# The closing norm of a decoder step: each chunk's norm formed under the next chunk's products, in three steps

## The chip, the cores and the metric

One core of a Trainium2 chip runs the whole program. The metric is device microseconds for one execution, from the first to the last instruction and what lies around them; lower is better. The core's engines work side by side, each through its own list of instructions in a fixed order: TensorE (PE) multiplies matrices into PSUM, VectorE (DVE) and GpSimd (POOL) do elementwise work, ScalarE (ACT) does functions and copies, and SyncE (SP) issues the transfers. An instruction that waits holds back everything behind it on its own engine.

## The reference

The program is one layer of a decoder for 1024 prompt tokens and 64 sample tokens (8 sequences of 8), followed by the final norm:

```python
def rms_norm(x, g):
    xf = x.astype(jnp.float32)
    y = xf * lax.rsqrt(jnp.mean(xf * xf, axis=-1, keepdims=True) + EPS)
    return (y * g.astype(jnp.float32)).astype(x.dtype)

def trunk_layer(x, ...):
    h = rms_norm(x, norm_mix_g)
    proj = h @ w_in
    ...                                   # convolution heads, attention heads
    x = x + jnp.concatenate([a, o], axis=-1) @ w_out
    h = rms_norm(x, norm_ffn_g)
    ...
    x = x + (jax.nn.silu(g) * (h @ w_ffn_up)) @ w_ffn_down
    return x, k, v, ...

y_prompt = rms_norm(xp, norm_final_g)
y_sample = rms_norm(xs, norm_final_g)
```

What matters here is the end: the product with `w_ffn_down`, the addition to `x`, and the last `rms_norm`, over 1024 features of each of 1088 tokens.

## The kernel before

Activations lie transposed: features on the 128 partitions (eight tiles `x2[0]` to `x2[7]`, one per 128 features, so `m` runs over 8), the 1088 tokens along the free axis. An f32 product is made of three matmuls: both operands are split into a rounded high part and the remainder (`whi`, `wlo`, `xh`, `xl`), and high times high, high times low and low times high are summed in one PSUM bank.

The product with `w_down` adds over 22 tiles of hidden features, in four groups (`GROUPS`). The first three groups go through `gemm` and are added to `x2`. The last group has two tiles from each half, so four activations, and goes through `last_product`. It takes the tokens in four chunks (`TAIL`: first token and width), and for each chunk the eight feature tiles `m` in turn. One product of a chunk is 12 matmuls into one PSUM bank; the tag `g` has 5 banks, which go round. Then, per `m`:

- DVE adds the bank to `x2[m]` (L1199), which frees the bank;
- ACT squares the sum (L1201) into a tile `sq`;
- the squares are added up over `m` (L1206): odd `m` on DVE, even `m` on POOL, in two running sums, which DVE joins at the end (L1207).

`last_norm` turns the summed squares of a chunk into output. `rstd` first multiplies the sum by a column of ones (L191, tag `r` in the trace), which adds over the partitions and leaves a token's sum in one partition; DVE, ACT and DVE make the inverse root of a few numbers (L193 to L206: tiles `rv`, `rr`, `rt`; L201 is the square root on ACT). Then PE transposes these, spread over 128 columns, back into rows of tokens (L213), and ACT copies them to SBUF (L215: tile `rb`). With `rb` the eight tiles of the chunk are scaled: even `m` by one instruction on DVE (L1215), odd `m` by a product on POOL (L1217) and a scaling on ACT (L1218). SP then issues the transfer of each (L1219).

The order of the work is set in two places. The code is written so that `last_norm` of a chunk comes behind `last_product` of the next chunk. A scheduler that works at build time then arranges each engine's list by what it reckons to be ready; the chip executes that list as it stands. The names `x_1742`, `x_1749`, `x_1774`, `x_1781`, `x_1788`, `x_1795`, `x_1802`, `x_1809` in the lists are `x2[0]` to `x2[7]`.

Of the kernel before, what the change touches and what calls it, by code (L numbers as in the profile page):

```python
# [21 lines left out]
ALU = mybir.AluOpType  # L22
PSUM = bass.MemoryType.PSUM

P = 128
D = 1024
# [4 lines left out]
N = S + NS  # L31
# [10 lines left out]
LN2 = float(np.log(2.0))  # L42
CHUNKS = ((0, 384), (384, 384), (768, 320))
GROUPS = ((0, 3), (3, 3), (6, 3), (9, 2))
TAIL = ((0, 256), (256, 256), (512, 320), (832, 256))
CH = 384
NCH = NCACHE // CH

# [23 lines left out]
C_GMIX, C_GFFN, C_GFIN = 0, 8, 16  # L72
# [5 lines left out]
def trunk_kernel(tc, xT, w_in, w_out, w_gate, w_up, w_down, par, kc, vc, sa, sf, pmask, smask,  # L78
                 yT, kT, vT, ca, cas, cf):
    nc = tc.nc  # L80
    with (
# [8 lines left out]
        def nm(s):  # L90
            cnt[0] += 1
            return f"{s}_{cnt[0]}"
# [20 lines left out]
        def bank(z, tag, bufs):  # L113
            return zone[z + "ps"].tile([P, 512], F32, tag=tag, name=nm(tag), bufs=bufs)
# [20 lines left out]
        def col(c):  # L135
            return prm[:, c:c + 1]
# [44 lines left out]

        rooted = [None]

        def rstd(sq, div, new, width=N):


            ps = bank(*rbank[0])
            nt = -(-width // P)
            size = [min(P, width - i * P) for i in range(nt)]
            for i, n in enumerate(size):  # L190
                nc.tensor.matmul(ps[:n, i:i + 1], sq[:, i * P:i * P + n], ones, start=True, stop=True)  # L191
            v = sp.tile([P, 9], F32, tag="rv", name=nm("rv"), bufs=2)[:, :nt]
            nc.vector.memset(v, 1.0)  # L193
            nf = width // P
            nc.vector.tensor_scalar(v[:, 0:nf], ps[:, 0:nf], 1.0 / div, EPS, op0=ALU.mult, op1=ALU.add)
            if nf < nt:
                n = size[-1]
                nc.vector.tensor_scalar(v[:n, nf:nt], ps[:n, nf:nt], 1.0 / div, EPS, op0=ALU.mult, op1=ALU.add)
            r = sp.tile([P, 9], F32, tag="rr", name=nm("rr"), bufs=2)[:, :nt]
            nc.vector.reciprocal(r, v)  # L200
            nc.scalar.activation(r, r, AF.Sqrt)  # L201

            t = sp.tile([P, 9], F32, tag="rt", name=nm("rt"), bufs=2)[:, :nt]
            nc.vector.tensor_mul(t, r, r)
            nc.vector.scalar_tensor_tensor(t, t, -0.5, v, op0=ALU.mult, op1=ALU.mult)
            rooted[0] = nc.vector.scalar_tensor_tensor(r, t, 1.5, r, op0=ALU.add, op1=ALU.mult).ins  # L206
            rb = new("rb")
            for c0 in range(0, width, 512):
                pb = bank(*rbank[0])
                w = min(512, width - c0)  # L210
                for i in range(c0 // P, -(-(c0 + w) // P)):
                    n = size[i]
                    nc.tensor.transpose(pb[:, i * P - c0:i * P - c0 + n], r[:n, i:i + 1].to_broadcast([n, P]),  # L213
                                        ident[:n, :n])
                nc.scalar.activation(rb[:, c0:c0 + w], pb[:, :w], AF.Copy)  # L215
            return rb

        def sum_squares(xs, eng, new, pool=()):
            acc = new("sqa")
            nc.scalar.activation(acc, xs[0], AF.Square)  # L220
            for i, x in enumerate(xs[1:]):
                s = new("sq")
                if i + 1 in pool:
                    nc.gpsimd.tensor_mul(s, x, x)
                else:
                    nc.scalar.activation(s, x, AF.Square)
                eng.tensor_add(acc, s, acc)
            return acc
# [517 lines left out]
        i = 0  # L746
        for p in range(NS1, NP):
            prompt_heads(i, HEADS[p - NS1])
            i = HEADS[p - NS1]
# [55 lines left out]
        for p, upto in zip(range(NS1, NP), SHEADS):  # L805
            prompt_heads(i, upto)
            i = max(i, upto)
# [46 lines left out]
        n = PARTS[-1]  # L854
# [11 lines left out]
        for m0 in (0, 4):  # L866
# [3 lines left out]
            for i in range(2):  # L870
                r = raw[:, i * 512:i * 512 + 512]
# [61 lines left out]
        for i in range(2):  # L933
            x = first_up[0][:, i * half:i * half + half]
# [5 lines left out]
        def out_half(h, hook):  # L940


            c = slice(h * HN, h * HN + HN)
            for m in range(KT):
                ps = pair()
                block_product(ps, wl[m], part[h], True)
                x = x2[m][:, c]
                added = nc.vector.tensor_add(x, all_of(ps), x).ins
                nc.sync.dma_start(x2d[m][:, c], x)
                s = slot("t1", "sq", F32)  # L950
                nc.scalar.activation(s, x, AF.Square)
                if m == 0:
                    acc = s
                else:
                    added = nc.vector.tensor_add(acc, s, acc).ins
                hook(m, added)
            return acc, added
# [5 lines left out]
        def norm_half(sq):  # L963
            return rstd(sq, D, lambda s: slot("t3", s, F32), HN)
# [16 lines left out]
        sq1, added = out_half(1, norm_first)  # L981
# [141 lines left out]
        def wide(s, dt=F32):  # L1123
            return zt("D", "X", ACTS, s, N, dt)
# [61 lines left out]
        nj = len(act)  # L1186


        def last_product(t0, n):
            acc = [None, None]  # L1190
            for m in range(KT):
                ps = bank(*gbank[0])
                whi, wlo = w[m]
                for k, (xh, xl) in enumerate(act):
                    nc.tensor.matmul(ps[:, :n], whi[:, k, :], xh[:, t0:t0 + n], start=(k == 0), stop=False)
                    nc.tensor.matmul(ps[:, :n], whi[:, k, :], xl[:, t0:t0 + n], start=False, stop=False)
                    nc.tensor.matmul(ps[:, :n], wlo[:, k, :], xh[:, t0:t0 + n], start=False, stop=(k == nj - 1))
                x = x2[m][:, t0:t0 + n]
                nc.vector.tensor_add(x, ps[:, :n], x)  # L1199
                s = wide("sq")[:, :n]  # L1200
                nc.scalar.activation(s, x, AF.Square)  # L1201
                i = m % 2
                if acc[i] is None:
                    acc[i] = s
                else:
                    (nc.vector if i else nc.gpsimd).tensor_add(acc[i], s, acc[i])  # L1206
            nc.vector.tensor_add(acc[0], acc[1], acc[0])  # L1207
            return acc[0]

        def last_norm(acc, t0, n):  # L1210
            R3 = rstd(acc, D, wide, n)[:, :n]
            for m in range(KT):
                x = x2[m][:, t0:t0 + n]
                if m % 2 == 0:
                    nc.vector.scalar_tensor_tensor(x, x, col(C_GFIN + m), R3, op0=ALU.mult, op1=ALU.mult)  # L1215
                else:
                    nc.gpsimd.tensor_mul(x, x, R3)  # L1217
                    nc.scalar.activation(x, x, AF.Copy, scale=col(C_GFIN + m))  # L1218
                nc.sync.dma_start(yT[m * P:(m + 1) * P, t0:t0 + n], x)  # L1219

        sums = []
        for i in range(len(TAIL)):
            sums.append(last_product(*TAIL[i]))
            if i:
                last_norm(sums[i - 1], *TAIL[i - 1])
        last_norm(sums[-1], *TAIL[-1])
        zd.__exit__(None, None, None)
        zr.__exit__(None, None, None)

# [91 lines left out]
```

## Time and profile before

| | us |
|---|---|
| median of three runs | 1429.69 (1428.96 to 1431.0) |
| the profiled execution's own time | 1432.72 |
| its span, first to last instruction | 1430.9 |
| products of the four chunks, within the span | 1362.25 to 1412.36 |
| behind the last product | 1412.36 to 1430.90 |

Times inside the span are read from its start. A row of the timeline gives start, duration, engine, source line, operation and shapes; equal neighbours are merged into one row with a count, and then the duration runs from the first one's start to the last one's end. What stands in brackets is the idle time before it and what ended it. A matmul's duration is longer than the distance to the next, because matmuls are pipelined: the distance is the pace.

### The profile page before, as it was taken

How to read it: one execution, taken by the hardware profiler on the slowest of the kernel's cores; microseconds unless marked ns; L12 is line 12 of the kernel's file. 1: busy time of each engine (PE TensorE's matmuls, PEld its weight loads, DVE VectorE, ACT ScalarE, POOL GpSimd, SP SyncE). 2: the span in 40 equal slices, each digit the busy share in tenths (PEclk: the TensorE clock that was granted, in tenths of full speed). 3: DMA queues.
4: the chain of work that ended last, by engine and by line, in shares of the span. 5: the costliest groups of instructions: out<-in, count | busy, mean ns of one | idle time of the engine just before them, and what ended most of it. 6: DMA issues, size and time to landing. Idle time of an engine off the chain costs nothing.

```text
span 1430.9 us, 24745 instructions
## 1 busy us (share of the span) xinstructions
PE 1350.0 (94%) x10011; PEld 1280.5 (89%) x10011; DVE 861.0 (60%) x1649; ACT 514.3 (36%) x982; POOL 431.5 (30%) x303
## 2 busy tenths in 40 slices
PE   6999999999999998976999999999999999999995
PEld 6988889999977777876899999999999889999995
DVE  7398595566574665679756566655656642423146
ACT  5312211457565564345333323333332321212033
POOL 3221111110000115231454445545445211224124
PEclk9999999999999998987999999999999999999998
DMA  7246676746699887340022122122212571414003
GB/s 271 54 139 245 226 255 206 206 141 179 180 276 226 243 228 225 112 162 8 30 91 91 65 87 91 52 70 91 91 62 91 167 291 45 139 48 131 11 9 118
DMA packets 84882, 195.16 MB, mean 136 GB/s; under 512 B 12576, under 2 KB 46752, under 8 KB 84768
## 3 DMA queue, kind: packets, MB, share of 16 engines
q1 hardware_dynamic: 84768, 193.57, 42.8%
q8 instruction: 79, 1.29, 0.4%
q14 instruction: 35, 0.29, 0.1%
HBM read 145.03 MB, written 48.52 MB: 135 GB/s over the span
## 4 chain that ended last, share of the span: by engine, by line
PE 76%; DVE 12%; DMA 6%; issue 2%; POOL 1%; ACT 1%; SPq 1%; POOLq 0%; ACTq 0%; DVEq 0%
PE g L174 9%; PE g L172 9%; PE g L173 9%; PE py L840 4%; PE py L842 4%; PE py L843 4%; DVE cacc L333 4%; PE o L666 3%; PE s L581 3%; PE pz L843 3%; PE pz L842 3%; PE pz L840 3%; PE px L843 3%; PE px L840 3%; PE px L842 3%; PE t L649 3%
## 5 line engine op out<-in xcount | busy, mean ns | idle before, releaser
L148 POOL TENSOR_TENSOR wl<-wr,wh 128x768 fp32r<-128x768 f32 (+2 forms) x61 | 117.1, 1921 | 464.7 <-PE g L174 391.8
L172 PE MATMUL g<-xh,wh 128*128 128x384 f32 (+1 forms) x472 | 158.6, 336 | 0.0
L173 PE MATMUL g<-xl,wh 128*128 128x384 f32 (+1 forms) x472 | 157.4, 333 | 0.0
L174 PE MATMUL g<-xh,wl 128*128 128x384 f32 (+1 forms) x472 | 157.2, 333 | 0.0
L172 PE MATMUL g<-ah,wh 128*128 128x384 f32 (+1 forms) x432 | 141.6, 333 | 5.0 <-ACT ah L1135 3.3
L173 PE MATMUL g<-al,wh 128*128 128x384 f32 (+1 forms) x432 | 143.0, 331 | 1.7 <-DVE al L1136 1.7
L174 PE MATMUL g<-ah,wl 128*128 128x384 f32 (+1 forms) x432 | 142.7, 331 | 0.7 <-POOL wl L148 0.7
L146 ACT ACTIVATE wh<-wr 128x768 fp32r<-128x768 f32 (+2 forms) x62 | 52.0, 838 | 241.0 <-PE g L174 177.5
L903 POOL TENSOR_TENSOR s<-wr,s 128x1024 fp32r<-128x1024 f32 x44 | 107.5, 2444 | 89.7 <-ACT s L902 47.9
L1158 DVE TENSOR_TENSOR x<-g,x 128x384 f32<-128x384 f32 (+1 forms) x72 | 38.0, 534 | 137.4 <-PE g L174 137.2
L622 ACT ACTIVATE y<-y,m 128x128 f32<-128x128 f32 (+1 forms) x192 | 88.4, 463 | 32.9 <-DVE m L610 32.9
L174 PEld LDWEIGHTS g<-xh,wl 128*128 128x128 f32 x472 | 90.0, 191 | 2.3 <-issue 2.1
L585 DVE CUSTOM_DVE_ANT_0 y<-s,pmk 128x128 f32<-128x128 f32 (+1 forms) x192 | 63.9, 378 | 45.8 <-PE s L581 36.9
L172 PEld LDWEIGHTS g<-xh,wh 128*128 128x128 f32 x472 | 90.1, 191 | 1.4 <-issue 1.2
L173 PEld LDWEIGHTS g<-xl,wh 128*128 128x128 f32 x472 | 90.0, 191 | 1.1 <-issue 1.0
L172 PEld LDWEIGHTS g<-ah,wh 128*128 128x128 f32 x432 | 82.0, 191 | 5.9 <-ACT ah L1135 3.6
L173 PEld LDWEIGHTS g<-al,wh 128*128 128x128 f32 x432 | 81.9, 190 | 2.0 <-DVE al L1136 2.0
L174 PEld LDWEIGHTS g<-ah,wl 128*128 128x128 f32 x432 | 81.8, 189 | 1.0 <-POOL wl L148 1.0
L333 DVE SCALAR_TENSOR_TENSOR cacc<-gp,prm,cacc 128x1024 f32<-128x1024 f32 x60 | 80.1, 1335 | 0.1
L1087 DVE SCALAR_TENSOR_TENSOR fc<-gb,prm,fc 128x1104 f32<-128x1104 f32 x44 | 79.0, 1813 | 2.0 <-ACT fc L1085 1.2
L903 POOL TENSOR_TENSOR wa<-wr,wa 128x1024 fp32r<-128x1024 f32 (+1 forms) x23 | 56.3, 2448 | 76.3 <-ACT wa L902 76.3
L381 DVE TENSOR_TENSOR qkv<-g,rb 128x384 f32<-128x384 f32 (+1 forms) x53 | 41.2, 777 | 46.0 <-PE g L174 45.9
(307 smaller groups left out, 4118.1 us busy)
## 6 DMA issues: line engine op xcount, KB each, us to landing
cr<-in_kc SPq DMA_DIRECT2D x24, 768.0 KB, 8.8
cr<-in_vc SPq DMA_DIRECT2D x24, 768.0 KB, 7.7
kk<-dk SPq DMA_DIRECT2D x48, 256.0 KB, 7.3
u<-u SPq DMA_DIRECT2D x22, 544.0 KB, 3.0
ur<-u SPq DMA_DIRECT2D x22, 544.0 KB, 4.8
wr<-in_w_in SPq DMA_DIRECT2D x22, 512.0 KB, 4.9
wr<-in_w_gate SPq DMA_DIRECT2D x22, 512.0 KB, 3.3
wr<-in_w_up SPq DMA_DIRECT2D x22, 512.0 KB, 4.5
```

What stands on the lines that cost most here:

```text
L148: lo_eng.tensor_sub(lo, raw, hi.bitcast(F32))
L172: nc.tensor.matmul(ps[c], whi[:, k, :], xh[:, t0:t0 + n], start=(k == 0), stop=False)
L173: nc.tensor.matmul(ps[c], whi[:, k, :], xl[:, t0:t0 + n], start=False, stop=False)
L174: nc.tensor.matmul(ps[c], wlo[:, k, :], xh[:, t0:t0 + n], start=False, stop=(k == nk - 1))
L333: eng.scalar_tensor_tensor(acc[:, :S], gp[:, j:j + S], col(w0 + j), acc[:, :S], op0=ALU.mult, op1=ALU.add)
L585: nc.vector.tensor_tensor_reduce(out=y[:, o:o + n], in0=ps[:, o:o + n], in1=mask, op0=ALU.add, op1=ALU.min, scale=1.0, scalar=3e38, accum_ ...
L622: nc.scalar.activation(y, y, AF.Exp, bias=m[:, 4 * g + i:4 * g + i + 1], scale=-1.0, accum_out=den[:, g, 2 * hd + u, i:i + 1])
L840: nc.tensor.matmul(ps, whi[:, k, :], xh[:, t], start=(start and k == 0), stop=False, skip_group_check=True)
L842: nc.tensor.matmul(ps, whi[:, k, :], xl[:, t], start=False, stop=False, skip_group_check=True)
L843: nc.tensor.matmul(ps, wlo[:, k, :], xh[:, t], start=False, stop=(k == nk - 1), skip_group_check=True)
L903: nc.gpsimd.tensor_sub(lo, x, hi.bitcast(F32))
L1087: nc.vector.scalar_tensor_tensor(c[:, :W], gb[i][:, t:t + W], col(C_FW + 3 * f + t), c[:, :W], op0=ALU.mult, op1=ALU.add)
```

## The change

The helper `rstd` is split in two: `root` (from the sum of squares to the inverse root of each token) and `spread` (the transposes and the copy to `rb`). `last_product` calls a hook behind each product, and the hook forms the norm of the chunk before: `root` behind product 0, `spread` and the scalings behind product 2, each held by `issue_after` behind the last matmul of that product on PE (an instruction may come later than that, not earlier). So the norm has three steps, inside the next chunk's products. The squares are summed in one running sum, all on DVE. The adds of the chunk (`m` above 2) are held behind a sum of squares from two products earlier, and for `m` above 3 behind the last scaling issued so far. For a chunk whose norm is formed under the next, POOL and ACT scale tiles 2 and 5 and DVE the other six; for the last chunk DVE scales all eight. The chunk of 320 tokens comes first instead of third.

```diff
-TAIL = ((0, 256), (256, 256), (512, 320), (832, 256))
+TAIL = ((0, 320), (320, 256), (576, 256), (832, 256))
...
-        def last_product(t0, n):
-            acc = [None, None]
+        def last_product(t0, n, hook):
+
+            acc = None
             for m in range(KT):
...
                 x = x2[m][:, t0:t0 + n]
-                nc.vector.tensor_add(x, ps[:, :n], x)
+                with ExitStack() as order:
+                    if m > 3 and scalings:
+                        order.enter_context(tc.issue_after(scalings[-1]))
+                    if m > 2:
+                        order.enter_context(tc.issue_after(added))
+                    nc.vector.tensor_add(x, ps[:, :n], x)
                 s = wide("sq")[:, :n]
                 nc.scalar.activation(s, x, AF.Square)
-                i = m % 2
-                if acc[i] is None:
-                    acc[i] = s
+                if m == 0:
+                    acc = s
                 else:
-                    (nc.vector if i else nc.gpsimd).tensor_add(acc[i], s, acc[i])
-            nc.vector.tensor_add(acc[0], acc[1], acc[0])
-            return acc[0]
-
-        def last_norm(acc, t0, n):
-            R3 = rstd(acc, D, wide, n)[:, :n]
+                    added, late = late if m > 1 else None, nc.vector.tensor_add(acc, s, acc).ins
+                hook(m, last.ins)
+            return acc
+
+        def scaled(R3, t0, n, others=()):
             for m in range(KT):
                 x = x2[m][:, t0:t0 + n]
-                if m % 2 == 0:
-                    nc.vector.scalar_tensor_tensor(x, x, col(C_GFIN + m), R3, op0=ALU.mult, op1=ALU.mult)
-                else:
+                if m in others:
                     nc.gpsimd.tensor_mul(x, x, R3)
                     nc.scalar.activation(x, x, AF.Copy, scale=col(C_GFIN + m))
+                else:
+                    scalings.append(nc.vector.scalar_tensor_tensor(x, x, col(C_GFIN + m), R3, op0=ALU.mult,
+                                                                   op1=ALU.mult).ins)
                 nc.sync.dma_start(yT[m * P:(m + 1) * P, t0:t0 + n], x)
...
+        acc = None
+        for i, (t0, n) in enumerate(TAIL):
+            r = []
+
+            def norm_of_last(m, last, acc=acc, r=r, chunk=TAIL[i - 1]):
+                if acc is None:
+                    return
+                with tc.issue_after(last):
+                    if m == 0:
+                        r.append(root(acc, D, chunk[1]))
+                    elif m == 2:
+                        scaled(spread(r[0], wide, chunk[1])[:, :chunk[1]], *chunk, others=(2, 5))
+
+            acc = last_product(t0, n, norm_of_last)
+        scaled(rstd(acc, D, wide, n)[:, :n], *TAIL[-1])
```

In the changed file the lines are numbered anew: the matmuls are L1207 to L1209, the add L1216, the square L1218, the sum of squares L1222, the scalings L1230 (POOL), L1231 (ACT) and L1233 (DVE), the transposes L221 and the multiplication by ones L194. Up to the first of the four chunks the engines' lists are those of before, but for the width of one memset.

The place where the lists differ most is the scaling. DVE's list before, inside the third chunk (320 wide), where the first chunk is scaled:

```order
L1199 TENSOR_TENSOR x_1774_12201<-g_14087,x_1774_12201 128x320 [waits PE_49]
L1215 SCALAR_TENSOR_TENSOR x_1742_12029<-x_1742_12029,prm,rb_14030 128x256 [waits Activation_49]
L1215 SCALAR_TENSOR_TENSOR x_1774_12201<-x_1774_12201,prm,rb_14030 128x256
L1215 SCALAR_TENSOR_TENSOR x_1788_12337<-x_1788_12337,prm,rb_14030 128x256
L1215 SCALAR_TENSOR_TENSOR x_1802_12473<-x_1802_12473,prm,rb_14030 128x256
L1199 TENSOR_TENSOR x_1781_12269<-g_14104,x_1781_12269 128x320 [waits PE_49]
```

Four scalings stand there between the adds of products 2 and 3. DVE's list now, inside the third chunk (256 wide), where the second chunk is scaled (`g_14159` is the bank of product 4, `g_14227` that of product 0 of the fourth chunk):

```order
L1216 TENSOR_TENSOR x_1781_12269<-g_14142,x_1781_12269 128x256 [waits PE_49]
...
L1233 SCALAR_TENSOR_TENSOR x_1742_12029<-x_1742_12029,prm,rb_14119 128x256 [waits Activation_49]
L1233 SCALAR_TENSOR_TENSOR x_1749_12097<-x_1749_12097,prm,rb_14119 128x256
L1233 SCALAR_TENSOR_TENSOR x_1781_12269<-x_1781_12269,prm,rb_14119 128x256
L1233 SCALAR_TENSOR_TENSOR x_1788_12337<-x_1788_12337,prm,rb_14119 128x256
L1233 SCALAR_TENSOR_TENSOR x_1802_12473<-x_1802_12473,prm,rb_14119 128x256
L1233 SCALAR_TENSOR_TENSOR x_1809_12541<-x_1809_12541,prm,rb_14119 128x256
L1222 TENSOR_TENSOR sq_14070<-sq_14156,sq_14070 128x256 [waits Activation_49]
L1216 TENSOR_TENSOR x_1788_12337<-g_14159,x_1788_12337 128x256 [waits PE_49]
L1216 TENSOR_TENSOR x_1795_12405<-g_14176,x_1795_12405 128x256 [waits PE_49]
L1216 TENSOR_TENSOR x_1742_12029<-g_14227,x_1742_12029 128x256 [waits PE_49]
```

The adds of products 4 to 7 of the chunk now stand behind six scalings, and the add of the next chunk's product 0 stands among them. PE's list now, at the same place (`g_14210` is the bank of product 7 of the third chunk, `g_14227` and `g_14256` those of products 0 and 1 of the fourth):

```order
L1207 MATMUL g_14210<-ah_13301,wh_13347 128x256 [waits DVE_49]
...
L1207 MATMUL g_14210<-ah_13313,wh_13347 128x256
L221 MATMUL r_14120<-ident,rr_14078 128x128 [waits DVE_49,Activation_49]
L221 MATMUL r_14120<-ident,rr_14078 128x128
L1208 MATMUL g_14210<-al_13314,wh_13347 128x256
...
L1207 MATMUL g_14227<-ah_13301,wh_13326 128x256
...
L1207 MATMUL g_14256<-ah_13301,wh_13326 128x256 [waits DVE_49]
```

The transposes stand behind 7 of the 12 matmuls of product 7, where the code asks for a place behind product 2 or later; in the second chunk they stand behind 4 of the 12 of product 6, in the fourth again behind 7 of product 7. With five banks, product 1 of the next chunk takes the bank that product 4 had, and waits for DVE's add of it.

More of the change, by code (lines that the diff above doesn't have):

```diff
@@ L182, in trunk_kernel, with sizes, root @@
         rooted = [None]
-        def rstd(sq, div, new, width=N):
+        def sizes(width):
+            return [min(P, width - i) for i in range(0, width, P)]
+        def root(sq, div, width):
             ps = bank(*rbank[0])
-            nt = -(-width // P)
-            size = [min(P, width - i * P) for i in range(nt)]
+            size = sizes(width)
+            nt = len(size)
             for i, n in enumerate(size):
@@ L206, in rstd, with spread @@
             rooted[0] = nc.vector.scalar_tensor_tensor(r, t, 1.5, r, op0=ALU.add, op1=ALU.mult).ins
+            return r
+        def spread(r, new, width):
+            size = sizes(width)
             rb = new("rb")
@@ L216, in rstd @@
             return rb
+        def rstd(sq, div, new, width=N):
+            return spread(root(sq, div, width), new, width)
         def sum_squares(xs, eng, new, pool=()):
@@ L1196, in last_product @@
                     nc.tensor.matmul(ps[:, :n], whi[:, k, :], xl[:, t0:t0 + n], start=False, stop=False)
-                    nc.tensor.matmul(ps[:, :n], wlo[:, k, :], xh[:, t0:t0 + n], start=False, stop=(k == nj - 1))
+                    last = nc.tensor.matmul(ps[:, :n], wlo[:, k, :], xh[:, t0:t0 + n], start=False, stop=(k == nj - 1))
                 x = x2[m][:, t0:t0 + n]
-                nc.vector.tensor_add(x, ps[:, :n], x)
+                with ExitStack() as order:
[4 more added lines that the diff above has]
+                    nc.vector.tensor_add(x, ps[:, :n], x)
@@ L1219, in last_norm @@
                 nc.sync.dma_start(yT[m * P:(m + 1) * P, t0:t0 + n], x)
[L1221 to L1226, printed above, removed]
+        scalings = []
+        acc = None
[10 more added lines that the diff above has]
+            acc = last_product(t0, n, norm_of_last)
```

## The prediction

> **What bounds the kernel now.** I read three views of the last 70 us, the only part whose lists differ: busy time by stage, the chain that ended last, and the timeline of single rows. The stages, cut where PE's chunks end, come first (columns: time, then PE, PEld, DVE, ACT, POOL busy, granted clock, transfers):
>
> ```profile
> 1362.25:1385.45 23.20, 23.20 (x197) 23.20 (x195) 9.33 (x22) 6.27 (x15) 4.03 (x6) 1.00 0.00 1
> 1385.45:1400.15 14.70, 14.70 (x104) 14.69 (x104) 9.52 (x22) 7.01 (x15) 5.79 (x8) 1.00 0.22 73
> 1400.15:1412.36 12.21, 12.21 (x106) 12.21 (x104) 8.40 (x21) 4.66 (x13) 5.77 (x7) 1.00 0.20 66
> 1412.36:1430.90 18.54, 2.34 (x15) 1.58 (x14) 11.34 (x24) 5.92 (x14) 8.10 (x9) 0.62 0.41 142
> ```
>
> While there are products, PE is busy the whole time and waits for nobody. Then 18.5 us follow in which it has almost nothing to do. The last matmul of the chunks (from the timeline), and the chain through the rest:
>
> ```profile
> 1412.07 0.28 PE L1197 MATMUL g<-ah,wl 128*128 128x256 f32 x1
> ```
>
> ```profile
> 1416.71 4.06 POOL x L1217 x4
> ...
> 1426.73 0.51 ACT x L1218
> ```
>
> The rest holds two norms one behind the other: the third chunk is scaled until 1420.8, then the fourth chunk's root is finished, and its scaling ends at 1427.2. From the last matmul's start to the end of the span it is 1430.9 - 1412.07 = 18.8 us. So two things count: when PE starts its last matmul (now 49.8 us behind the first, 1412.07 - 1362.25), and what comes behind that.
>
> **What a scaling costs.** The clearest place is the second chunk's:
>
> ```profile
> 1405.25 0.28 PE L1196 MATMUL g<-al,wh 128*128 128x256 f32 x1
> 1405.37 0.38 PE L213 MATMUL r<-ident,rr 128*128 128x128 f32 x2
> 1405.51 0.37 PE L1197 MATMUL g<-ah,wl 128*128 128x256 f32 x1
> 1405.71 0.29 PE L1195 MATMUL g<-ah,wh 128*128 128x256 f32 x1
> ...
> 1405.79 0.39 ACT L215 ACTIVATE rb<-r 128x256 f32<-128x256 f32 x1 [4.41 <-PE r L213]
> 1406.20 3.70 DVE L1215 SCALAR_TENSOR_TENSOR x<-x,prm,rb 128x256 f32<-128x256 f32 x4 [0.81 <-ACT rb L215]
> 1409.83 0.41 DVE L1199 TENSOR_TENSOR x<-g,x 128x256 f32<-128x256 f32 x1
> 1406.25 3.38 POOL L1217 TENSOR_TENSOR x<-x,rb 128x256 f32<-128x256 f32 x4 [5.32 <-ACT rb L215]
> 1412.54 0.74 DVE L1199 TENSOR_TENSOR x<-g,x 128x256 f32<-128x256 f32 x2
> L961 DVE SCALAR_TENSOR_TENSOR x<-x,prm,rb 128x544 f32<-128x544 f32 x16 | 11.4, 779 | 0.0
> ```
>
> From the transposes to the first scaling it takes 0.83 us (1405.37 to 1406.20). With POOL working beside it, DVE needs 3.63 us for four scalings, 0.91 each. A scaling of 256 alone does not occur. Bounds: 0.33, the step between two adds of that width (0.74 - 0.41), and 0.91 as above. The nearest row is the same operation alone at 544 columns, 11.4 / 16 = 0.71 a step; cut down between the add's 0.33 and that, I take 0.37 for 256, by the same way 0.43 for 320. So six scalings, two of them beside POOL's two, take 2 x 0.91 + 4 x 0.37 = 3.3 us.
>
> **The change, part by part.**
>
> *More in PE's stream.* A sum by ones and two transposes now stand inside the products for three chunks, before for two.
>
> ```profile
> 1385.17 0.28 PE L1197 MATMUL g<-ah,wl 128*128 128x256 f32 x1
> 1385.65 0.39 PE L1195 MATMUL g<-ah,wh 128*128 128x320 f32 x1
> 1385.88 0.31 PE L1196 MATMUL g<-al,wh 128*128 128x320 f32 x1
> 1385.49 0.42 DVE L1199 TENSOR_TENSOR x<-g,x 128x256 f32<-128x256 f32 x1 [1.02 <-PE g L1197]
> 1386.46 0.43 DVE L1206 TENSOR_TENSOR sq<-sq,sq 128x256 f32<-128x256 f32 x1 [0.27 <-ACT sq L1201]
> ```
>
> The matmul pace at 256 is 0.12 (1405.25 to 1405.37). The sums take 1385.17 to 1385.65, 0.36 more than a step, and the step behind them is slow by some 0.1; the transposes take 0.14 more (1405.25 to 1405.51) and 0.08 behind. One more of each is 0.7; the 320 chunk's norm has three columns instead of two, half as much again of its own share, 0.3. Together +1.0 us. The chunk widths only change places: nothing.
>
> *The wait of PE at the head of the fourth chunk.* This is the step on which the sign rests: the adds of products 4 to 7, which free the banks, stand on DVE behind the six scalings, and these behind the transposes. Let B be the start of the third chunk's transposes. PE: 0.14 + 0.20 + 4 x 0.12 for the rest of product 7 (0.82), 12 x 0.12 for the next product 0, so at B + 2.3 it stands before product 1, whose bank is that of product 4. DVE: first scaling at B + 0.83, six take 3.3, one sum of squares 0.34, then the add of product 4, 0.42: B + 4.9. PE starts again some 0.15 later (below, DVE's last root step to the transposes). The wait is 5.0 - 2.3 = 2.7 us. Behind the scalings are queued four adds; ACT's squares wait for them; everything is late together.
>
> *The same at the head of the third chunk.* There the transposes stand behind 4 matmuls of product 6 and the scaled chunk is 320 wide. PE reaches product 1 at B + 0.25 + 0.2 + 7 x 0.12 + 2 x 1.44 = B + 4.2. DVE:
>
> ```profile
> 1415.56 0.60 PE L213 MATMUL r<-ident,rr 128*128 128x128 f32 x3 [2.66 <-DVE rr L206]
> 1416.20 0.44 ACT L215 ACTIVATE rb<-r 128x320 f32<-128x320 f32 x1 [2.30 <-PE r L213]
> 1416.73 0.16 DVE L195 TENSOR_SCALAR rv<-r 128x2 f32<-128x2 f32 x1 [1.32 <-PE r L191]
> 1416.81 4.31 DVE L1215 SCALAR_TENSOR_TENSOR x<-x,prm,rb 128x320 f32<-128x320 f32 x4
> 1421.04 0.15 DVE L200 RECIPROCAL rr<-rv 128x2 f32<-128x2 f32 x1
> ```
>
> Three transposes to POOL's first scaling 1.15 us (1415.56 to 1416.71; that holds a cold step, so I take 1.05); two scalings beside POOL 1.06 each (4.23 / 4), four at 0.43, one sum, one add: B + 1.05 + 2.1 + 1.7 + 0.8 + 0.1 = B + 5.75. The wait is 1.5 us. The second chunk's head has no norm ahead of it, so no wait.
>
> So PE's last matmul starts 1.0 + 1.5 + 2.7 = 5.2 us later than now.
>
> *Behind the last matmul.* Call its start Q. The third chunk's transposes stand five matmuls before the end, at Q - 0.7, so its six scalings begin only at Q + 0.13 and end at Q + 3.4. Nine DVE steps of the last chunk are queued behind them: sum 3, adds 4 to 7, sums 4 to 7. At 0.34 that is 3.1; the first and the last sum wait for ACT's square (above, add to sum 1385.49 to 1386.46, 0.97 instead of two steps, 0.3 each): Q + 7.1. Then the fourth chunk's own norm, by the rows of before:
>
> ```profile
> 1416.09 0.60 PE L191 MATMUL r<-ones,sq 128*128 128x1 f32 x4
> ...
> 1421.86 0.16 DVE L206 SCALAR_TENSOR_TENSOR rr<-rt,rr 128x2 f32<-128x2 f32 x1
> ...
> 1422.16 0.66 PE L213 MATMUL r<-ident,rr 128*128 128x128 f32 x2 [5.47 <-DVE rr L206]
> 1422.92 0.38 ACT L215 ACTIVATE rb<-r 128x256 f32<-128x256 f32 x1 [0.58 <-PE r L213]
> 1423.34 3.65 DVE L1215 SCALAR_TENSOR_TENSOR x<-x,prm,rb 128x256 f32<-128x256 f32 x4 [1.32 <-ACT rb L215]
> ...
> 1425.28 3.28 SPq L1219 DMA_DIRECT2D out_yT<-x  x7
> ```
>
> Sum by ones to scaling: 0.64 (1416.09 to 1416.73), 0.2, and 2.3 (1421.04 to 1423.34) without the 4.2 of scaling that stands between now: 3.1, plus 0.3 because PE has been idle longer. First scaling at Q + 10.6. All eight are on DVE, alone, at 0.37 a step; SP issues slower, seven in 3.28, 0.48 a step. So the first issue starts 0.45 later, the last 7 x 0.48 behind it: Q + 14.4. The last issue now starts at 1428.56 - 0.40 = 1428.16, 2.74 before the end. End at Q + 17.2, against 18.8: 1.6 us less.
>
> *What costs nothing.* The root's small steps on DVE and ACT, the square root's table load among them, are over before PE reaches the transposes, three products behind the sum by ones. POOL's twelve additions of squares move to DVE, 12 x 0.34 = 4 us; in the first three chunks DVE is busy 9.3 of 23.2 us, and in the fourth they are counted among the nine steps. The 24 transfers of the first three chunks now go in order of `m`, so those of tiles 3 and 4 wait for tile 2 through POOL and ACT; SP has over 10 us between chunks, and nobody waits for them.
>
> **The sum.** +1.0 + 1.5 + 2.7 - 1.6 = +3.6 us against the profiled execution's 1432.72 (span 1430.9), so 1436.3 there. That execution lies 3.0 above the median of 1429.69; against the median the forecast is 1433.3, 0.25% slower. A measurement of this kernel tells about 0.2% (2.9 us) from no change, so the forecast lies just beyond that.
>
> **The rivals.**
>
> *DVE and POOL do not hold each other up.* If a mix of six and two ran at 0.37 throughout, six scalings would take 2.2 instead of 3.3. That is 1.1 less at three places: +0.3, 1430.0, no change. It decides where a scaling beside POOL falls under 0.65. Against it: the four that took 3.63 with POOL's four in the same stretch, and 4.23 at 320.
>
> *The norm comes as early as the code allows.* If the transposes ran right behind product 2, the scalings would be over before product 6 ends, PE would not run out of banks, and the last chunk's sums would be up to date at its end. Then add to sum 1.8 (1385.17 to 1386.89 and a step to PE), 3.4 to the first scaling, 0.45 + 3.4 + 2.7: Q + 11.8, and in all +1.0 - 7.0 = -6.0: 1423.7, faster. It decides where the transposes stand ahead of product 4. Against it: PE's list, which has them in products 6 and 7, and the chip follows the list.
>
> *PE comes back slow from its wait.* The two stretches behind the products:
>
> ```profile
> 1412.40:1416.00 3.60, 0.94 (x8) 0.70 (x7) 2.71 (x11) 0.84 (x3) 0.72 (x1) 1.00 0.21 73
> 1416.00:1422.00 6.00, 0.70 (x5) 0.54 (x5) 4.93 (x9) 2.33 (x6) 4.06 (x4) 0.57 0.39 137
> ```
>
> After an idle stretch of 2.66 us the clock is still 1.00, in the next one it falls to 0.57. My second wait of 2.7 us lies just at the first. If it tips, one to two products run at half pace, 1.4 to 2.9 us more: 1434.7 to 1436.2. It decides at an idle time between 2.66 and 5.47.
>
> The Trainium skill, "TensorE: Matmul & The Clock Gate", section "What's actually happening", has PE at half clock after an idle window of about 3.4 us, whose phase is free. By that rule a wait of 2.7 us costs nothing and the sum stays; no run yet shows a wait in between.
>
> **How the numbers follow.** The forecast's mechanism, waits at two heads and a shorter end, 0.82. Its size moves with twelve lone scalings (0.33 to 0.45 each, -0.5 to +1.0), the place where the waits begin and the scatter of runs (1428.96 to 1431.0): about 1430.8 to 1435.5. I put 0.54 of it beyond +0.2%, 0.28 within. No blocking: 0.07, within. Early norm: 0.04, faster; a broad misreading of the end's chain, 0.01, also faster. Slow PE: 0.06, slower. Together: faster 0.05, within 0.2% 0.35, slower 0.60. The range for 8 in 10 goes from 1430.2, near the case without blocking, to 1435.8, into that of the slow clock.
>
> **What would show it.** PE idle in front of product 1 of the third and fourth chunk, by 1.5 and 2.7 us, released by DVE's add; in the first chunks none. Scalings of 0.37 a step when alone. The third chunk's scalings starting where the products end, about 55 us behind the first matmul. Last matmul to end 17.2 us, the last eight issues on SP without a gap. I am wrong if PE shows no such wait, or if DVE finishes the last sum within 4 us of the last matmul.

## The result and the profile after

| | before | after |
|---|---|---|
| median of 5 runs each, same chip | 1429.69 (1426.64 to 1432.71) | 1435.36 (1434.81 to 1436.82) |
| ratio | 1 | 1.0041 (95%: 1.0023 to 1.0060) |
| the profiled execution's own time, its span | 1432.72, 1430.9 | 1436.82, 1435.0 |
| first matmul of the four chunks | 1362.25 | 1358.97 |
| from there to the last matmul of the chunks | 49.8 | 58.4 |
| from there to the end of the span | 18.8 | 17.6 |

The change made the kernel slower by 0.41%, inside the forecast range and near its upper end (1433.3, range 1430.2 to 1435.8). Measured again, it came out 0.55% slower (below), which would lie beyond that end.

The two profiles must not be compared by their spans. The lists ahead of the four chunks are the same in both, but that part came out 3.3 us shorter in the second execution, and over all the profiles of this study the first matmul of the chunks lies between 1351.4 and 1363.5. What the change does is read from the first matmul of the chunks to the end of the span. I call this stretch the gauge: 68.7 us before, 76.1 after. It grew by 7.4 us, not by the forecast 3.6.

The stages after, from the first matmul of the chunks to PE's first wait, to its second, to the last matmul, to the end (columns as in the prediction's first table):

```profile
1358.97:1387.23 28.26, 28.26 (x214) 27.99 (x213) 14.18 (x34) 8.39 (x17) 1.97 (x2) 1.00 0.02 7
1387.23:1401.08 13.85, 12.43 (x105) 12.23 (x103) 8.40 (x26) 4.00 (x11) 1.20 (x2) 1.00 0.24 84
1401.08:1417.41 16.33, 13.61 (x92) 13.41 (x91) 8.53 (x25) 3.80 (x11) 0.41 (x1) 0.79 0.19 65
1417.41:1435.05 17.64, 1.93 (x9) 1.29 (x7) 10.74 (x28) 3.67 (x10) 1.59 (x2) 0.58 0.35 119
```

In the first row PE is busy throughout. In the second and third 1.4 and 2.7 us are missing, and in the third the granted clock is 0.79. The waits of PE within the chunks are one line:

```profile
PE g L1207 <- DVE x L1216: 4.1, 2, 2.7
```

Two waits for a bank that DVE's add frees, and no other. Their places in PE's timeline:

```profile
1387.23 0.28 PE L1209 MATMUL g<-ah,wl 128*128 128x256 f32 x1
1388.93 0.39 PE L1207 MATMUL g<-ah,wh 128*128 128x256 f32 x1 [1.42 <-DVE x L1216]
1389.15 0.28 PE L1208 MATMUL g<-al,wh 128*128 128x256 f32 x1
...
1401.08 0.28 PE L1209 MATMUL g<-ah,wl 128*128 128x256 f32 x1
1404.08 0.58 PE L1207 MATMUL g<-ah,wh 128*128 128x256 f32 x1 [2.72 <-DVE x L1216]
1404.46 0.42 PE L1208 MATMUL g<-al,wh 128*128 128x256 f32 x1
1404.67 0.41 PE L1209 MATMUL g<-ah,wl 128*128 128x256 f32 x1
...
1409.79 0.41 PE L1209 MATMUL g<-ah,wl 128*128 128x256 f32 x1
1410.01 0.32 PE L1207 MATMUL g<-ah,wh 128*128 128x256 f32 x1
1410.16 0.27 PE L1208 MATMUL g<-al,wh 128*128 128x256 f32 x1
```

The bracket counts idle time from the modelled end of the last matmul, which overlaps the next one; the loss is the distance of the two starts less one step of 0.12: 1388.93 - 1387.23 - 0.12 = 1.58, and 1404.08 - 1401.08 - 0.12 = 2.88. DVE's timeline ahead of the second wait's end:

```profile
1399.83 3.52 DVE L1233 SCALAR_TENSOR_TENSOR x<-x,prm,rb 128x256 f32<-128x256 f32 x6 [3.44 <-ACT rb L223]
1403.28 0.41 DVE L1222 TENSOR_TENSOR sq<-sq,sq 128x256 f32<-128x256 f32 x1
1403.61 1.07 DVE L1216 TENSOR_TENSOR x<-g,x 128x256 f32<-128x256 f32 x3
```

The chain is the forecast one: six scalings, a sum, then the add (1403.61) for which PE stands. What the forecast sum does not hold follows the second wait: steps of 0.21 instead of 0.12 (1404.46 to 1404.67) up to 1410.0, 27 matmuls in all. After the first wait the pace is normal.

DVE's timeline behind the last matmul:

```profile
1417.60 3.50 DVE L1233 SCALAR_TENSOR_TENSOR x<-x,prm,rb 128x256 f32<-128x256 f32 x6 [3.45 <-ACT rb L223]
...
1424.27 0.42 DVE L1222 TENSOR_TENSOR sq<-sq,sq 128x256 f32<-128x256 f32 x1 [0.21 <-ACT sq L1218]
...
1428.37 3.25 DVE L1233 SCALAR_TENSOR_TENSOR x<-x,prm,rb 128x256 f32<-128x256 f32 x8 [1.32 <-ACT rb L223]
```

With the last matmul at 1417.41, the third chunk's scalings start 0.19 behind it, the last sum ends 7.3 behind it, the final scalings start 11.0 behind it. SP's last eight issues start 0.48 apart (1428.88 to 1432.25), without a gap, as forecast.

### The profile page after: what moved, and what is told of

Its sections match the earlier page's. It is cut to its first block, busy times and chain, and to the rows that moved or that the text cites. A ratio compares the mean times of both kernels' runs of the same rounds, so it can differ in the third digit from the quotient of the medians.

```text
span 1435.0 us, 24732 instructions
## 1 busy us (share of the span) xinstructions
PE 1354.5 (94%) x10011; PEld 1284.0 (89%) x10011; DVE 865.1 (60%) x1671; ACT 510.0 (36%) x972; POOL 413.5 (29%) x281
## 4 chain that ended last, share of the span: by engine, by line
PE 76%; DVE 14%; DMA 6%; issue 2%; ACT 1%; SPq 1%; POOL 1%; DVEq 0%; ACTq 0%; POOLq 0%
PE g L174 9%; PE g L172 9%; PE g L173 9%; PE py L851 4%; PE py L853 4%; PE py L854 4%; DVE cacc L344 4%; PE o L677 3%; PE pz L854 3%; PE pz L853 3%; PE pz L851 3%; PE s L592 3%; PE px L854 3%; PE px L851 3%; PE px L853 3%; PE t L660 2%
```

## The experiments

The theory: the transposes stand late in PE's list, so six scalings stand on DVE ahead of the adds that free PE's banks; PE waits for these, and the longer wait lets its clock fall. The rivals: another part of the change costs the time (one sum on DVE, six scalings on DVE, the chunk order), or the slow matmuls have another cause. All ratios are to the kernel before, run beside. "Gauge" is from each kernel's own profile.

| | time, us | ratio (95%) | first to last matmul | last matmul to end | gauge |
|---|---|---|---|---|---|
| before | | 1 | 49.8 | 18.8 | 68.7 |
| the change | 1435.36 | 1.0041 (1.0023 to 1.0060) | 58.4 | 17.6 | 76.1 |
| again | 1437.26 | 1.0055 (1.0033 to 1.0077) | 55.8 | 17.6 | 73.5 |
| early transposes | 1427.65 | 0.9978 (0.9956 to 1.0001) | 52.2 | 12.8 | 65.0 |
| filled wait | 1432.41 | 1.0032 (1.0009 to 1.0054) | 55.8 | 17.1 | 72.9 |
| order and sum only | 1427.09 | 0.9985 (0.9964 to 1.0005) | 50.5 | 18.4 | 68.9 |
| 32 columns | 1432.77, one run | | 52.3 | 16.2 | 68.6 |
| all on DVE | 1435.81, one run | | 56.6 | 16.1 | 72.7 |
| early, two queues | 1424.61 | 0.9962 (0.9945 to 0.9979) | 51.6 | 11.8 | 63.4 |
| early, two queues, no POOL | 1420.79 | 0.9947 (0.9927 to 0.9967) | 51.4 | 11.9 | 63.3 |

**The change again.** No edit.

> The changed kernel once more, unaltered. Gauge, beside the time: from the first matmul of the four chunks to the end of the span (before 68.7 us, the profiled execution after 76.1 us). If the slow matmuls behind the second wait belong to the change, they are there again: a wait of 2.7 to 3.0 us at the head of the fourth chunk, some 27 matmuls at 0.21 us, gauge 75.5 to 76.5, time 5 to 6.5 above before. If they were an accident of that one execution, the gauge is about 73.5 and the time 3.3 to 4 above before.

The two waits are the same to 0.01 us, but the slow matmuls are not there:

```profile
1405.62 0.28 PE L1209 MATMUL g<-ah,wl 128*128 128x256 f32 x1
1408.62 0.39 PE L1207 MATMUL g<-ah,wh 128*128 128x256 f32 x1 [2.72 <-DVE x L1216]
1408.85 0.28 PE L1208 MATMUL g<-al,wh 128*128 128x256 f32 x1
1408.96 0.28 PE L1209 MATMUL g<-ah,wl 128*128 128x256 f32 x1
```

The same wait of 2.88 us, a step of 0.11 to 0.12 behind it. The gauge is 73.5, the first profile's less 2.6. So the waits are there in both profiled executions of the change, the fall of the clock in only one. The median stands 8.6 us above before all the same: five rounds tell this kernel's time to about 0.2%, and the gauge is the finer tool.

**Early transposes.** The next product's matmuls are held behind the transposes, and these behind product 3 (`at`: 4 in the second chunk); the sum by ones stands likewise right behind product 1. `placed[0]` is the last matmul of the sum by ones, or the last transpose.

```diff
+                    if m in held:
+                        order.enter_context(tc.issue_after(held[m]))
                     for k, (xh, xl) in enumerate(act):
...
-                    if m == 0:
+                    if m == 1:
                         r.append(root(acc, D, chunk[1]))
-                    elif m == 2:
-                        scaled(spread(r[0], wide, chunk[1])[:, :chunk[1]], *chunk, others=(2, 5))
+                        held[m + 1] = placed[0]
+                    elif m == at:
+                        rb = spread(r[0], wide, chunk[1])
+                        held[m + 1] = placed[0]
+                        scaled(rb[:, :chunk[1]], *chunk, others=(2, 5))
```

> The change with the transposes held in their place on PE: right behind product 3 (second chunk: product 4) instead of inside products 6 and 7. Theory (the late transposes put the six scalings ahead of DVE's adds, so PE runs out of banks, and its clock falls in the wait): no wait over 0.3 us at the heads of the third and fourth chunk, no slow matmuls, last product's sums up to date when PE ends; first to last matmul about 51 us, last matmul to end about 12 to 14 us, gauge 63 to 65, time 4 to 6 below before (ratio 0.996 to 0.997). Rival (the cost lies in the other parts: all sums and six of eight scalings on DVE, the 320 chunk first): the placement of the transposes changes little, gauge 73 or more, time not below before.

The theory holds for the waits. PE no longer waits for a bank; one gap of 0.9 us is left, before the third chunk's sum by ones, which PE reaches a little before DVE has the sum (timeline):

```profile
1391.63 0.58 PE L196 MATMUL r<-ones,sq 128*128 128x1 f32 x4 [0.77 <-DVE sq L1228]
```

The stretches up to the last matmul and behind it, columns as before:

```profile
1360.88:1413.08 52.20, 51.43 (x407) 50.98 (x405) 35.41 (x91) 18.11 (x42) 5.20 (x6) 1.00 0.17 57
1413.08:1425.85 12.77, 1.82 (x9) 1.19 (x7) 6.24 (x19) 1.84 (x6) 0.00 (x0) 0.61 0.36 123
```

Against the change without slow matmuls, the late place costs 73.5 - 65.0 = 8.5 us: 3.6 in the products, 4.8 behind them. The sums on DVE, the six scalings and the chunk order are all still there. The measured time moved less than expected, 0.2% under before, with an interval that just touches 1.

**Filled wait.** `fill`, 22 in the fourth chunk, matmuls that nobody reads stand in the second wait.

```diff
+                if m == 0 and fill:
+                    pf = zone["Dps"].tile([P, 512], F32, tag="f", name=nm("f"), bufs=1)
+                    with tc.issue_after(last.ins):
+                        for _ in range(fill):
+                            filler = nc.tensor.matmul(pf[:, :n], w[0][0][:, 0, :], act[0][0][:, t0:t0 + n], start=True, stop=True).ins
```

> The changed kernel, with 22 matmuls of 128x256 into a bank of their own, read by nobody, put on PE between products 0 and 1 of the fourth chunk, where it waits 2.9 us. They take 22 x 0.12 = 2.6 us, so PE is idle for less than 0.5 us there. If the slow matmuls behind that wait come from PE having been idle, they go: pace 0.12 throughout, gauge about 73.5 (76.1 less 2.6), time 2 to 3 below the unaltered change. Rival (the pace falls for another reason, contention for PSUM or what DVE does then): 27 matmuls at 0.21 remain, gauge 76 or more.

PE's timeline at the filled place (L1219 the filling):

```profile
1402.54 2.80 PE L1219 MATMUL f<-ah,wh 128*128 128x256 f32 x22
1405.42 0.39 PE L1211 MATMUL g<-ah,wh 128*128 128x256 f32 x1
1405.64 0.28 PE L1212 MATMUL g<-al,wh 128*128 128x256 f32 x1
1405.76 0.28 PE L1213 MATMUL g<-ah,wl 128*128 128x256 f32 x1
```

The pace stays 0.12 and the gauge is 72.9 (0.6 of it because the fourth chunk's transposes stand 5 matmuls earlier here). But the unaltered change has shown the same pace without filling, so one profile settles nothing about the clock. That was left to the two measurements below.

**Order and sum only.** The kernel before with the 320 chunk first and one sum of squares on DVE.

```diff
-TAIL = ((0, 256), (256, 256), (512, 320), (832, 256))
+TAIL = ((0, 320), (320, 256), (576, 256), (832, 256))
...
-                    (nc.vector if i else nc.gpsimd).tensor_add(acc[i], s, acc[i])
-            nc.vector.tensor_add(acc[0], acc[1], acc[0])
-            return acc[0]
+                    nc.vector.tensor_add(acc, s, acc)
+            return acc
```

> The kernel before with only two parts of the change: the 320 chunk first, and the squares in one sum on DVE. The norm stays behind the next chunk's products, with four scalings on DVE and four on POOL and ACT. Theory (the late norm costs the time): no wait at the heads, gauge 66.5 to 69, time 0 to 2 below before. Rival (these two parts cost the time): waits or a longer end already here, gauge 72 or more, time 3 to 6 above before.

No wait, gauge 68.9 against 68.7, and a time that cannot be told from before. These parts cost nothing and bring nothing that can be told from the noise: the cost lies in where the norm stands.

**The scalings on 32 columns.** The first three chunks' scalings on DVE are cut to 32 columns; the rest of those tiles goes out unscaled.

```diff
+                    e = n if not others else 32
-                    scalings.append(nc.vector.scalar_tensor_tensor(x, x, col(C_GFIN + m), R3, op0=ALU.mult, op1=ALU.mult).ins)
+                    scalings.append(nc.vector.scalar_tensor_tensor(x[:, :e], x[:, :e], col(C_GFIN + m), R3[:, :e], op0=ALU.mult, op1=ALU.mult).ins)
```

> The changed kernel, but DVE's six scalings of the first three chunks cover 32 columns instead of 256 or 320 (the rest of those tiles goes out unscaled). The transposes of the second and third chunk stand 4 matmuls (0.5 us) earlier, else the lists are the same. Theory (PE waits for adds that are queued behind six scalings): six scalings take about 1.2 us instead of 3.4, so the wait at the third chunk's head is gone, that at the fourth's is under 0.5; first to last matmul about 51.5 (unaltered 55.8), last matmul to end about 15.4 (17.6), gauge about 67. Rival (the wait comes from what stands ahead of the scalings, transposes and copy): waits of 1.0 and 2.3 stay, gauge 71 or more.

DVE's and POOL's scalings ahead of the fourth chunk's head in the timeline, then PE there:

```profile
1401.08 2.17 DVE L1234 SCALAR_TENSOR_TENSOR x<-x,prm,rb 128x32 f32<-128x32 f32 x6 [3.44 <-ACT rb L223]
1401.12 1.43 POOL L1230 TENSOR_TENSOR x<-x,rb 128x256 f32<-128x256 f32 x2 [11.98 <-ACT rb L223]
```

```profile
1402.80 0.28 PE L1209 MATMUL g<-ah,wl 128*128 128x256 f32 x1
1403.97 0.39 PE L1207 MATMUL g<-ah,wh 128*128 128x256 f32 x1 [0.89 <-DVE x L1216]
```

The first wait is gone; the second is 1403.97 - 1402.80 - 0.12 = 1.05, not under 0.5. What was wrong was the price of six small scalings, 2.1 us and not 1.2: the two that run beside POOL take 0.75 and 0.70 a step at 32 columns, the other four 0.16. The wait follows this price: the scalings became 3.42 - 2.10 = 1.3 shorter and the transposes moved 0.5 ahead, and the wait fell by 2.88 - 1.05 = 1.83. That is the theory's chain, measured link by link; the rival's 2.3 did not stay.

**All scalings on DVE.**

```diff
-                        scaled(spread(r[0], wide, chunk[1])[:, :chunk[1]], *chunk, others=(2, 5))
+                        scaled(spread(r[0], wide, chunk[1])[:, :chunk[1]], *chunk)
```

> The changed kernel with all eight scalings of every chunk on DVE, none on POOL and ACT; the lists are otherwise the same. Theory (DVE and POOL hold each other up): eight alone take 8 x 0.396 = 3.2 us, less than six with POOL beside them (3.4), and at 320 3.7 against 4.1; waits at the heads 1.1 to 1.2 and 2.6, gauge 72.4 to 72.8 without slow matmuls, about 75 with them. Rival (they don't): the two scalings that DVE does more cost 0.8 at each place: waits 2.4 and 3.7, gauge 75.5 or more.

DVE's scalings of the first two chunks, and PE at the fourth chunk's head, in the timeline:

```profile
1386.27 3.79 DVE L1233 SCALAR_TENSOR_TENSOR x<-x,prm,rb 128x320 f32<-128x320 f32 x8 [2.48 <-ACT rb L223]
1401.69 3.26 DVE L1233 SCALAR_TENSOR_TENSOR x<-x,prm,rb 128x256 f32<-128x256 f32 x8 [3.44 <-ACT rb L223]
1402.94 0.28 PE L1209 MATMUL g<-ah,wl 128*128 128x256 f32 x1
1405.67 0.39 PE L1207 MATMUL g<-ah,wh 128*128 128x256 f32 x1 [2.46 <-DVE x L1216]
...
1406.01 0.41 PE L1209 MATMUL g<-ah,wl 128*128 128x256 f32 x1
1406.23 0.42 PE L1207 MATMUL g<-ah,wh 128*128 128x256 f32 x1
```

Eight scalings alone are over in 3.26 us, six with two beside POOL in 3.52. The waits are 1.16 and 2.61, as the theory said. Here the clock fell again, for 16 matmuls, after a wait that is shorter than the one that left it alone in the second execution of the change. The gauge came out at 72.7 rather than 75 with slow matmuls for two reasons: 16 slow matmuls cost 1.5 us and not the 2.6 of 27, and the lists were not otherwise the same, as I had written: in the fourth chunk the transposes stand 11 matmuls (1.3 us) earlier, and the end is shorter by about that.

**The clock by itself.** Twice the kernel before got a second part behind its end: bursts of matmuls, with waits between them of a length that DVE sets. `pf` is a PSUM bank of its own, `seen` a tile that nobody reads.

```diff
+        for rep in range(6):
+            for k in (4, 6, 7, 8, 9, 10, 12):
+                for b in range(64):
+                    nc.tensor.matmul(pf[:, :256], w[0][0][:, 0, :], act[0][0][:, :256], start=True, stop=True)
+                for b in range(k):
+                    nc.vector.tensor_copy(seen[:, :256 - 8 * rep], pf[:, :256 - 8 * rep])
```

> The kernel before, with a measurement behind its end that adds to its time and to none of its results: 42 times, 64 matmuls of 128x256 into one bank, then 4, 6, 7, 8, 9, 10 or 12 copies of that bank by DVE, for which the next 64 matmuls wait; six rounds of the seven lengths. PE is thus idle for about 1.8, 2.5, 2.8, 3.2, 3.5, 3.8 and 4.5 us. Asked: after which idle times does the pace fall from 0.12, and for how long. Theory (a clock that looks at windows whose phase is free, of a length below 2.9 us): none slow at 1.8, some but not all slow near 2.9, a growing share above, and a slow stretch of about 5 to 6 us each time. Rival from the stated window of 3.4 us: none slow at 2.5, 2.8 and 3.2, the first ones at 3.5 or above. Rival (idleness alone does not do it): none slow at any length.

The length of a wait does not decide. Of five waits of 1.9 to 2.0 us three were followed by slow matmuls, of six of 2.7 to 3.0 one, and of six of 3.1 to 3.4 all. But the moments at which the granted clock changes all lie on one grid of 3.413 us, in this trace and in the others: in the change's profile it falls at 1403.24, comes back at 1410.07 and falls again at 1420.31, two and three times 3.413 apart. So I sorted by windows of this grid. Idle time is counted here as what the distance between two starts has beyond one step (0.12, in a slow window 0.21). After 32 windows with up to 1.84 us of idle PE the next was fast, after 31 with over 2.02 it was slow, none the other way; of four between 1.93 and 2.02 one was followed by a slow one. Both rivals fall, and so does the expectation's window of under 2.9 us.

The second measurement asked whether the idle time must be in one piece:

```diff
+            for parts in ((3,), (3, 3), (5,), (2, 2), (6,), (2, 2, 2)):
+                burst(64 + 5 * rep)
+                for j, k in enumerate(parts):
+                    if j:
+                        burst(6)
+                    for b in range(k):
+                        nc.vector.tensor_copy(seen[:, :256 - 8 * rep], pf[:, :256 - 8 * rep])
```

> The kernel before with a second measurement behind its end: bursts of 64 to 94 matmuls, and between them waits of PE for 3, 5 or 6 copies by DVE (about 1.5, 2.4 and 2.8 us), or for 2 + 2, 3 + 3 and 2 + 2 + 2 copies with 6 matmuls (0.7 us) in between. Theory (windows of 3.413 us, the next one slow if the idle time within one adds up to about 1.9 us or more): 1.5 alone never slow; 2.4 and 2.8 in over half of the cases; 3 + 3 (two idles of 1.5 in 3.7 us) slow in over half although neither idle alone is; 2 + 2 (two of 1.1 in 2.9 us) slow in some; and each case told right by the idle time in its window. Rival (one unbroken idle of 1.9 us or more within a window is needed): 3, 3 + 3, 2 + 2 and 2 + 2 + 2 never slow.

Three windows of its grid, each with the window behind it (busy time of PE, count, granted clock; busy counts each matmul to its modelled end, so what is left of the window is less than the idle time as counted above):

```profile
1629.47:1632.88 3.41, 1.96 (x12) 1.00 0.00 0
1632.88:1636.30 3.42, 2.55 (x21) 1.00 0.00 0
1537.31:1540.72 3.41, 1.54 (x13) 1.00 0.00 0
1540.72:1544.14 3.42, 3.42 (x19) 0.50 0.00 0
1796.72:1800.14 3.42, 1.60 (x11) 1.00 0.01 2
1800.14:1803.55 3.41, 2.50 (x12) 0.50 0.00 0
```

In the first, 1.98 us of idle time leave the clock at 1.00. In the second, 1.99 us, nearly all in one piece, halve it for the next window; these two lie at the border. In the third two pieces, the longer of 1.07 us, and the slower steps behind them add up to 2.20 and halve it too. Over the whole run: 47 windows with up to 1.88 us idle were followed by a fast one, 22 with over 2.02 by a slow one, none the other way, and the first two shown are the only ones between. Of the 23 that were followed by a slow one 14 had no piece over 1.6 us. The rival (one unbroken idle) falls. One expectation missed: of seven single waits of 2.3 to 2.5 us two were followed by slow matmuls, not over half. Of seven of 2.7 to 3.0 all were, against one of six in the first measurement: the phase decides, not the length. To come back, PE must be busier: in both measurements a slow window with up to 0.73 idle was followed by a fast one, with 0.80 or more by another slow one.

The grid explains the profile of the change. Its windows around the second wait, and two of the second execution:

```profile
1399.83:1403.24 3.41, 1.53 (x13) 1.00 0.25 87
1403.24:1406.65 3.41, 2.57 (x12) 0.50 0.66 221
1406.65:1410.07 3.42, 3.42 (x18) 0.50 0.00 0
1410.07:1413.48 3.41, 3.41 (x31) 1.00 0.02 5
```

```profile
1404.25:1407.67 3.42, 1.65 (x14) 1.00 0.23 78
1407.67:1411.08 3.41, 2.46 (x20) 1.00 0.68 230
```

In the change's first profile the wait lies from 1401.20 to 1404.08, so 2.04 us of it fall into the first window: just enough. The second is slow and, with 1.0 idle, too idle to end it; the third is slow throughout. In the second execution the same wait lies from 1405.74 to 1408.62. 1.92 us of it fall into the first window, and with the slow step behind it 1.1 us of idle time into the next: neither held enough, by a narrow margin.

**A version that beats both.** The early placement, with the transposes behind product 3 in the second chunk also, and the last chunk's transfers on two queues.

```diff
-                nc.sync.dma_start(yT[m * P:(m + 1) * P, t0:t0 + n], x)
+                (nc.scalar if not others and m % 2 else nc.sync).dma_start(yT[m * P:(m + 1) * P, t0:t0 + n], x)
```

> The early placement, with the transposes behind product 3 in the second chunk also, and the last chunk's transfers issued in turn by SP and ACT. Theory: no waits for banks at the heads; last matmul to end 11.8 to 12.2 (12.8 with SP alone), since eight issues of 0.48 on one queue are slower than eight scalings of 0.4; gauge 63 to 64, time 4 to 6 below before, ratio 0.996 to 0.997. Rival (transfers, not their issue, set the end): last matmul to end stays 12.8, gauge 64.5 to 65.

The stretches up to the last matmul and behind it:

```profile
1360.15:1411.71 51.56, 51.41 (x406) 50.97 (x405) 35.34 (x91) 18.17 (x42) 5.21 (x6) 1.00 0.17 57
1411.71:1423.52 11.81, 1.52 (x9) 0.88 (x7) 6.25 (x19) 1.85 (x6) 0.00 (x0) 0.69 0.40 133
```

The gap before the sum by ones is gone, and the kernel is 0.38% faster than before (0.21 to 0.55). The end is 11.8 instead of 12.8: the first of the final scalings starts 5.8 us behind the last matmul instead of 6.1, and from there to the end it takes 6.0 instead of 6.7. That last 0.7 is the second queue's; that the transfers and not their issue set the end (the rival) does not hold. The last variant takes POOL out of the scaling as well (`others=()`):

> The early placement with two queues, and all scalings of all chunks on DVE: POOL and ACT scale nothing. Theory (beside POOL a scaling on DVE lasts as long as POOL's): eight alone take 3.2 us, less than six with two on POOL (3.4), so the adds behind them come 0.25 us sooner at each place, the last sums too; last matmul to end 11.5 to 11.8 (11.8), gauge 62.7 to 63.4 (63.4), ratio to before 0.9955 to 0.997. Rival (DVE becomes the bound, since it now does everything): waits at the heads, or a last sum later than now; gauge 64 or more.

Gauge 63.3 against 63.4, end 11.9 against 11.8: no difference. The eight scalings are 0.2 us shorter (3.25 against 3.46 for six), but nothing waits for them any more. Its ratio of 0.9947 is the best; its interval overlaps that of the variant with POOL, and the gauge shows no gain.

## Why the prediction was right, and where it was off

| step of the prediction | predicted | measured |
|---|---|---|
| PE's wait at the head of the third chunk | 1.5 | 1.58 |
| PE's wait at the head of the fourth | 2.7 | 2.88 |
| more in PE's stream | 1.0 | 1.5 |
| last matmul to end (before: 18.8) | 17.2 | 17.6 |
| first final scaling, behind the last matmul | 10.6 | 11.0 |
| last sum ends, behind the last matmul | 7.1 | 7.3 |
| a scaling of 256 alone | 0.37 | 0.40 |
| sum, without slow matmuls | +3.6 | +4.8 |
| slow clock after the second wait | a rival, 1.4 to 2.9, chance 0.06 | 2.6 in one profile, 0 in another |

The mechanism that the sign rested on is there, at the forecast places, released by the forecast instruction; 32 columns showed that the wait follows the scalings, and early transposes that it goes with the place. A norm under the next products brought only 1.2 us at the end because most of it did not lie under them: the transposes stood so late that the last chunk's nine DVE steps ended 7.3 us behind the last matmul. With the transposes held in their place the end was 12.8, 6 us shorter than before.

Two terms were too small. *More in PE's stream* missed 0.5 us: each restart after a wait costs a step of 0.22 instead of 0.12, twice, and the norm of 320 columns holds PE twice as long as one of 256 (1.35 us against 0.67), not half as long again. The end missed 0.4: the last sum ended 0.2 later, with scalings of 0.40 rather than 0.37 ahead of it, and the way from there through the root took 3.7 instead of 3.4.

The rival that DVE and POOL do not hold each other up is refuted at both widths. The rival of the early norm did not happen in this change. Its sign was right and its price too large: it gave -6.0, and the early version's gauge is 68.7 - 65.0 = 3.7 shorter, with the products 2.4 longer rather than 1.0 and an end of 12.8 rather than 11.8. Two queues, which the rival did not have, make it 5.3.

The step that failed is the clock. I put it at 0.06 because I read the rows of before as a wait of 2.66 that had left the clock at 1.00 and one of 5.47 that made it fall, and took the threshold for a length between the two. That reading was wrong for those rows already. The 0.57 is a mean over 6 us; the clock fell at 1416.84, when the wait of 5.47 had lasted 0.15 us (PE in two windows of the grid, before):

```profile
1413.43:1416.84 3.41, 1.14 (x7) 1.00 0.00 0
1416.84:1420.25 3.41, 0.00 (x0) 0.50 0.25 89
```

Of the wait of 2.66 (1412.90 to 1415.56) 2.13 us lie in the first of these windows, enough by themselves: a wait as long as the forecast one had already been followed by the slow clock. The threshold is a share of a window with a free phase. With about 2.0 of 3.41 us needed in one window, a wait of 2.88 escapes only if both its parts stay below that, which leaves 2 x 2.0 - 2.88 = 1.1 us of 3.41 for its start: by this estimate about one execution in three. Each slow window costs 3.41 x (1 - 0.12 / 0.21) = 1.5 us, at times nearly two of them. So the estimate is some 1.0 us on average, and the sum would have been +5.8. The first measurement gave +5.7, the second, by its ratio of 1.0055, +7.9 with an interval from +4.7 to +11.0. That the first fell inside a range made for +3.6 is in part luck. The estimate rests on the two measurements of the clock; how often the changed kernel itself runs slow was seen in two profiles only. The Trainium skill, "TensorE: Matmul & The Clock Gate", section "What's actually happening", speaks of an idle window of about 3.4 us. The length of the window and its free phase agree with these runs (3.413, and from the span's start the grid lies 1.01 us later in the second profile of the change than in the first); that PE must be idle for the whole of it does not: a little over 2.0 us, even in two pieces, were enough. The measurement decides.

## What to carry to other kernels

Work that is meant to lie under another stage must be held there from both sides: a rule that only says "not earlier" lets a scheduler put it late, and then it stands ahead of what the next stage waits for. Before moving elementwise work onto the engine that frees the matmul's banks, count how many banks' worth of matmuls (here 4 x 1.44 us) pass between its place and the first matmul that needs one. When a wait of PE remains, price it at its length plus the chance that it fills more than half of a clock window.

## What the runs showed that I had not expected

- PE's clock is set by windows of 3.413 us: in both measurements the next one ran at half clock whenever PE was idle for over 2.02 us in this one, never up to 1.88, whether or not in one piece. Coming back took a window with at most 0.73 idle; with 0.80 it did not.
- A scaling on DVE beside a product on POOL lasts about as long as POOL's: 0.75 us at 32 columns, which alone take 0.16. Cutting DVE's operand does not help there; eight scalings on DVE alone (3.26) end before six with POOL's help (3.52).
- Transfers issued by one queue at 0.48 us each set the end when the scalings come every 0.40: a second queue brought 0.7 us.
